# Six weight-half buffers at places of their own modulo 128 bytes, and MLP activations 1024 bytes apart

## The chip, the cores and the metric

The kernel runs on one NeuronCore of a Trainium2 chip. The metric is the device time of one execution in microseconds, as the median of several executions. The profile shown here is one further execution, taken by the hardware profiler.

Names of engines: PE (TensorE: matmuls, and "PEld", its weight loads), DVE (VectorE), ACT (ScalarE), POOL (GpSimd), SP (SyncE, which here only issues DMAs). SBUF is the on-chip memory of 128 partitions; an address below is a byte address within a partition. PSUM holds matmul results.

## The reference

One encoder block over a batch of one, 256 tokens of width 2048. Only the matrix products matter for this change:

```python
mod = jax.nn.silu(c) @ w_ada[l] + b_ada[l]
h = modulate(rms_norm(x, g_norm1[l]), sh1, sc1)
... = jnp.split(h @ w_in[l], IN_SPLITS, axis=-1)      # 2048 -> 7184 columns
...                                                   # mLSTM heads, neighbourhood attention
mixed = jnp.concatenate([h_a, h_b], axis=-1) @ w_out[l]   # 2048 -> 2048
x = x + ga1[:, None, :] * mixed
h = modulate(rms_norm(x, g_norm2[l]), sh2, sc2)
u, g = jnp.split(h @ w_up, 2, axis=-1)                # 2048 -> 2 x 5632
g = ...                                               # depthwise conv of width 3
x = x + ga2 * ((gelu(g) * u) @ w_down)                # 5632 -> 2048
```

Everything is float32 and the result must have float32 accuracy.

## The kernel before

**Split products.** A float32 product is computed from two halves of each operand. `wh` is the weight rounded to the PE's fp32r type, `wl = w - wh` is the rest; an activation is split the same way into `hh` and `hl` (in the down-projection: `aTh` and `aTl`). Each tile product is three one-pass matmuls: high weight by high activation, high weight by low activation, low weight by high activation (L394, L395, L396 in `mm_w`). In `mm_w` the weight slice of 128x128 is the operand that is loaded into the array (PEld) and the activation, 128x256, is the moving operand that streams through it. In `mm_x` (L401 to L403, used only for the two value projections) it is the other way round: the activation is loaded and a row of the weight half, 128x512, streams.

**The weight stream.** All of `w_in`, `w_out`, `w_up` and `w_down` pass once through SBUF, in 391 pieces of up to 128x1024 floats. The class `Stream` does for each piece: SP issues the DMA into a raw buffer `wr` (L349), ACT makes `wh` by a rounding copy (L359), DVE makes `wl` by a subtraction (L367), PE runs the piece's matmuls (24 for most), and then the pair of halves is free again. There are three `wh` and three `wl` buffers (`WH_BUFS = 3`): ACT may be at most three pieces ahead of PE. In this version each trio is a ring of three buffers of 4096 bytes.

**The stages in order.** First `w_in` (until about 388 us of the profile), with the mLSTM and attention work beside it; then `w_out` (to about 487 us); then the up-projection (`second_half`, 4224 matmuls of form L394 to L396 with 256 columns); then the down-projection (`rows` with `down_steps`), from 972 us to 1220 us, and a short tail. In the down-projection 44 activation tiles of 128x256 meet four groups of output columns. The first 40 of them (`n_own`) lie in two large tiles, `aTh` and `aTl`, in which a row is `S + STEP = 260` floats, that is 1040 bytes from one activation to the next. The last four lie in the rings `hh` and `hl`, 1024 bytes apart, as all activations of the earlier stages do. Beside the weight stream runs the modulation matrix `w_ada`, streamed on POOL's queue and reduced on DVE, until about 720 us.

**What sets the order.** A planner (`Sched`) decides at build time in which order each engine's instructions stand. It uses durations and due times, and no addresses.

**Places.** A pool lays its tiles out one after the other, in the order in which they are first asked for. `shift`, a tile of 64 bytes at the start of `wpool`, moves all that follows by 64 bytes. The lines that the change touches:

```python
SHIFT = 16
STEP = 4
wh = self.view(wpool.tile([P, PIECE], F32R, name="wh", tag="wh", bufs=WH_BUFS), nk)
wl = self.view(wpool.tile([P, PIECE], F32R, name="wl", tag="wl", bufs=WH_BUFS), nk)
aTh = upool.tile([P, n_own, S + STEP], F32R, name="aTh")
```

Of the kernel before, what the change touches and what calls it, by code (L numbers as in the profile page):

```python
# [8 lines left out]
F32R = mybir.dt.float32r  # L9
# [5 lines left out]
P = 128  # L15
D = 2048
KT = D // P
S = 256
# [8 lines left out]
FT = FF // P  # L27
# [14 lines left out]
WH_BUFS = 3  # L42
# [26 lines left out]
SEEDS = (0, 1, 1, 1, 1)  # L69
CH = 512  # L70
SHIFT = 16
STEP = 4
PIECE = 1024

CHUNK_COLS = {}
# [69 lines left out]
def block_kernel(ctx, tc, xT_d, cols_d, bg_d, rpb_d, ada_d, win_d, wg_d, wout_d, wup_d, wdown_d, const_d, out_d):  # L145
# [6 lines left out]
    wpool = ctx.enter_context(tc.tile_pool(name="wpool", bufs=1))  # L152
# [22 lines left out]
    class Sched:  # L175
        LAT = {"PE": 0.2, "DVE": 0.14, "ACT": 0.14, "SP": 0.0, "POOL": 0.0}

        def __init__(self):
            self.clock = {"PE": 0.0, "DVE": 0.0, "ACT": 0.0, "SP": 0.0, "POOL": 0.0}
            self.dma_free = 0.0  # L180
            self.chains = []
            self.now = 0.0
            self.slack = 0
# [63 lines left out]
    def held(what):  # L247
        return any(a in flags and b not in flags and what in c for a, b, c in HOLDS)
# [4 lines left out]
    def dve(n, *conds):  # L253
        return "DVE", 0.07 + n / 960, conds

    def act(n, *conds):
        return "ACT", 0.1 + n / 1210, conds
# [65 lines left out]


    class Stream:
        def __init__(self):
            self.todo, self.raw, self.cut, self.half = [], {}, {}, {}
            self.at = {}
            self.pos = 0
            self.wr, self.wh = Ring("wr", WR_BUFS, WR_EARLY), Slots(WH_BUFS)  # L330
# [21 lines left out]
        def cutting(self):  # L352
            for i, (_, _, nk) in enumerate(self.todo):
                n = nk * CH
                t = yield act(n, lambda: self.raw[i][1] if i in self.raw else None, self.wh.has())
                self.wh.take()
                raw = self.view(self.raw[i][0], nk)
                wh = self.view(wpool.tile([P, PIECE], F32R, name="wh", tag="wh", bufs=WH_BUFS), nk)
                A.copy(wh, raw)  # L359
                self.half[i] = (raw, wh, t)  # L360

        def rest(self):
            for i, (_, _, nk) in enumerate(self.todo):
                t = yield dve(nk * CH, lambda: self.half[i][2] if i in self.half and not held("r") else None)
                raw, wh, _ = self.half.pop(i)
                wl = self.view(wpool.tile([P, PIECE], F32R, name="wl", tag="wl", bufs=WH_BUFS), nk)
                V.tensor_sub(wl, raw, wh.bitcast(F32))  # L367
                self.raw.pop(i)[2].give(t)
                self.cut[i] = (wh, wl, t)
# [825 lines left out]
    upool = ctx.enter_context(tc.tile_pool(name="upool", bufs=1))  # L1195
# [1 line left out]
    aslots, gslots = Slots(3), Slots(GC_BUFS)  # L1197
    h2 = [None] * KT
    n_own = FT - CH // P
    aTh = upool.tile([P, n_own, S + STEP], F32R, name="aTh")  # L1200
    aTl = upool.tile([P, n_own, S + STEP], F32R, name="aTl")
    aT = [(aTh[:, j, :S], aTl[:, j, :S]) for j in range(n_own)] + [None] * (FT - n_own)
    cw0, cb0 = NCOL["cw"][0], NCOL["cb"][0]
    gated = {}

# [225 lines left out]
```

## Time and profile before

| what | value |
|---|---|
| median of 3 executions | 1239.87 us |
| lowest, highest | 1239.19, 1254.86 us |
| the profiled execution, its own time | 1237.55 us |
| its span, first to last instruction | 1235.8 us |
| mean granted TensorE clock in it | 0.992 |
| instructions | 24381 |
| weights and other data read from HBM | 318.85 MB |

The page of the profile gives the busy time of each engine, the same in 40 slices of the span, the DMA queues, the chain of work that ended last, and the costliest groups of instructions. A group's line reads: line of the kernel, engine, operation, output and inputs, shapes, count, then the busy time in us and the mean duration of one in ns, and behind the bar the idle time of the engine just before these instructions and what ended it. Matmuls overlap: one of 256 columns is listed with some 277 ns, yet the next one starts after 113 ns or so. What PE costs is therefore read from the distance of the starts, or from the number of matmuls in a stretch of time (a stretch counts the two that reach into it from before as well). The modelled end of a matmul moves with the start of the next, so the listed duration still shows where the distance grows.

### The profile page before, as it was taken

The numbers are of one execution on the slowest core, as the hardware profiler recorded it, in microseconds if no ns is written. First come the engines' busy times: TensorE is split into PE (matmuls) and PEld (weight loads), VectorE is DVE, ScalarE is ACT, GpSimd is POOL, SyncE is SP. The second block draws the span as 40 slices with busy tenths as digits, with TensorE's granted clock in tenths as the row PEclk, the third lists the DMA queues.
The fourth block names the chain that finished last, engine by engine and source line by source line (L and its number), as shares of the span: only waits on it lengthen the run. The fifth ranks groups of instructions, "written<-read, shape, count | busy, mean of one in ns | idle before, by whom it ended". The sixth has DMA issues, their size and how long they took to land.

```text
span 1235.8 us, 24381 instructions
## 1 busy us (share of the span) xinstructions
PE 1208.4 (98%) x9822; PEld 1171.7 (95%) x9822; DVE 906.3 (73%) x1382; ACT 682.9 (55%) x1027; POOL 110.5 (9%) x208
## 2 busy tenths in 40 slices
PE   8899999999999998999999999999999999999996
PEld 6789999999989998999999999999999999999995
DVE  5999889889999998997666676766766545454543
ACT  5896667758777444555445454544555434343432
POOL 1111111122112211010000000000000000000000
PEclk9999999999999999999999999999999999999998
DMA  8999989998998997797777777767666655655552
GB/s 311 402 373 356 331 298 379 374 298 264 323 311 272 380 348 283 255 372 242 228 231 240 232 228 231 243 226 225 217 190 192 197 184 188 186 188 186 184 187 85
DMA packets 91313, 322.55 MB, mean 261 GB/s; under 512 B 10560, under 2 KB 11072, under 8 KB 91200
## 3 DMA queue, kind: packets, MB, share of 16 engines
q1 hardware_dynamic: 63360, 220.84, 52.3%
q0 software_dynamic: 27840, 100.15, 24.0%
q8 instruction: 77, 1.26, 0.4%
q14 instruction: 36, 0.29, 0.1%
HBM read 318.85 MB, written 2.10 MB: 260 GB/s over the span
## 4 chain that ended last, share of the span: by engine, by line
PE 93%; DMA 3%; ACT 2%; DVE 1%; SPq 0%; issue 0%; DVEq 0%; ACTq 0%
PE acc_u L395 13%; PE acc_u L396 13%; PE acc_u L394 13%; PE acc_r L395 9%; PE acc_r L394 9%; PE acc_r L396 9%; PE acc L394 5%; PE acc L395 5%; PE acc L396 5%; PE acc L403 2%; PE acc L402 2%; PE acc L401 2%; DMA wre<-in_win 2%; PE bank L893 1%; ACT wh L359 1%; DMA wr<-in_win 1%
## 5 line engine op out<-in xcount | busy, mean ns | idle before, releaser
L367 DVE TENSOR_TENSOR wl<-wr,wh 128x1024 fp32r<-128x1024 f32 (+1 forms) x391 | 466.6, 1194 | 260.0 <-ACT wh L359 259.0
L359 ACT CAST wh<-wr 128x1024 fp32r<-128x1024 f32 (+1 forms) x391 | 402.0, 1028 | 426.4 <-PE acc_u L395 196.5
L394 PE MATMUL acc_u<-hh,wh 128*128 128x256 f32 x1408 | 389.8, 277 | 3.4 <-ACT hh L435 3.4
L395 PE MATMUL acc_u<-hl,wh 128*128 128x256 f32 x1408 | 389.7, 277 | 0.1
L396 PE MATMUL acc_u<-hh,wl 128*128 128x256 f32 x1408 | 389.4, 277 | 0.0
L394 PEld LDWEIGHTS acc_u<-hh,wh 128*128 128x128 f32 x1408 | 265.2, 188 | 3.9 <-ACT hh L435 3.9
L395 PEld LDWEIGHTS acc_u<-hl,wh 128*128 128x128 f32 x1408 | 265.2, 188 | 0.4 <-DVE hl L437 0.4
L396 PEld LDWEIGHTS acc_u<-hh,wl 128*128 128x128 f32 x1408 | 265.2, 188 | 0.0
L394 PE MATMUL acc<-hh,wh 128*128 128x256 f32 x640 | 182.9, 286 | 6.8 <-ACT hh L435 2.3
L394 PE MATMUL acc_r<-aTh,wh 128*128 128x256 f32 x640 | 180.2, 282 | 0.0
L395 PE MATMUL acc_r<-aTl,wh 128*128 128x256 f32 x640 | 179.7, 281 | 0.0
L396 PE MATMUL acc_r<-aTh,wl 128*128 128x256 f32 x640 | 179.4, 280 | 0.0
L395 PE MATMUL acc<-hl,wh 128*128 128x256 f32 x640 | 178.1, 278 | 0.1
L396 PE MATMUL acc<-hh,wl 128*128 128x256 f32 x640 | 178.0, 278 | 0.0
L465 POOL DMA_DIRECT2D ar<-in_ada x173 | 91.7, 530 | 682.4 <-DVE modp L492 334.4
L394 PEld LDWEIGHTS acc<-hh,wh 128*128 128x128 f32 x640 | 121.0, 189 | 12.4 <-ACT acc L263 4.3
L395 PEld LDWEIGHTS acc<-hl,wh 128*128 128x128 f32 x640 | 121.0, 189 | 1.1 <-DVE are L460 0.3
L396 PEld LDWEIGHTS acc<-hh,wl 128*128 128x128 f32 x640 | 121.1, 189 | 0.0
L395 PEld LDWEIGHTS acc_r<-aTl,wh 128*128 128x128 f32 x640 | 120.5, 188 | 0.1
L396 PEld LDWEIGHTS acc_r<-aTh,wl 128*128 128x128 f32 x640 | 120.6, 188 | 0.0
L394 PEld LDWEIGHTS acc_r<-aTh,wh 128*128 128x128 f32 x640 | 120.4, 188 | 0.1
L492 DVE CUSTOM_DVE_ANT_0 ar<-ar,srow,modp 128x1024 f32<-128x1024 f32 x87 | 111.2, 1278 | 1.6 <-DMA ar<-in_ada 1.4
(202 smaller groups left out, 1562.7 us busy)
## 6 DMA issues: line engine op xcount, KB each, us to landing
wr<-in_wup SPq DMA_DIRECT2D x176, 512.0 KB, 3.9
ar<-in_ada POOLq DMA_DIRECT2D x173, 512.0 KB, 6.1
wr<-in_wdown SPq DMA_DIRECT2D x88, 512.0 KB, 3.5
wr<-in_win SPq DMA_DIRECT2D x73, 512.0 KB, 6.3
wr<-in_wout SPq DMA_DIRECT2D x32, 512.0 KB, 6.3
wre<-in_win SPq DMA_DIRECT2D x25, 512.0 KB, 5.7
are<-in_ada POOLq DMA_DIRECT2D x15, 512.0 KB, 6.2
wr<-in_win SPq DMA_DIRECT2D x22, 256.0 KB, 5.4
```

The source lines that it names most:

```text
L359: A.copy(wh, raw)
L367: V.tensor_sub(wl, raw, wh.bitcast(F32))
L394: T.matmul(acc[:, n, :], w_h, h[0], start=st, stop=False, skip_group_check=True)
L395: T.matmul(acc[:, n, :], w_h, h[1], start=False, stop=False, skip_group_check=True)
L396: T.matmul(acc[:, n, :], w_l, h[0], start=False, stop=last, skip_group_check=True)
L401: T.matmul(acc[:, t, :], h_h, wh[:, k, :], start=first, stop=False, skip_group_check=True)
L402: T.matmul(acc[:, t, :], h_h, wl[:, k, :], start=False, stop=False, skip_group_check=True)
L403: T.matmul(acc[:, t, :], h_l, wh[:, k, :], start=False, stop=last, skip_group_check=True)
L465: q.dma_start(raw, ada_d[a : a + P * PIECE].rearrange("(p n) -> p n", p=P))
L492: V.tensor_tensor_reduce(raw, raw, srow[:, h * PIECE : (h + 1) * PIECE], 1.0, modp[:, part, k : k + 1] if h else cols[:, c : c + 1], ALU.m ...
L893: T.matmul(nu[1][:, : DH_A + 1], at[d][:, j, :], va[:, u, h, :], start=n == 0, stop=n == len(blocks) - 1)
```

## The change

The two rings become six tiles with a buffer each, `wh0` to `wh2` and `wl0` to `wl2`, taken in turn by the new method `half_tile`. Each is 16 floats longer than a piece, and the piece starts in it after 0, 8, 12 or 16 floats by the table `OFFS`. `aTh` and `aTl` lose the four spare floats of each row.

```diff
-STEP = 4
+OFFS = {"wh": (0, 8, 8), "wl": (16, 12, 12)}
+PAD = 16
...
     class Stream:
+        def half_tile(self, what):
+            q = self.turn[what]
+            self.turn[what] = (q + 1) % WH_BUFS
+            o = OFFS[what][q]
+            return wpool.tile([P, PIECE + PAD], F32R, name=f"{what}{q}", tag=f"{what}{q}", bufs=1)[:, o : o + PIECE]
+
...
+            self.turn = {"wh": 0, "wl": 0}
...
-                wh = self.view(wpool.tile([P, PIECE], F32R, name="wh", tag="wh", bufs=WH_BUFS), nk)
+                wh = self.view(self.half_tile("wh"), nk)
...
-                wl = self.view(wpool.tile([P, PIECE], F32R, name="wl", tag="wl", bufs=WH_BUFS), nk)
+                wl = self.view(self.half_tile("wl"), nk)
...
-    aTh = upool.tile([P, n_own, S + STEP], F32R, name="aTh")
-    aTl = upool.tile([P, n_own, S + STEP], F32R, name="aTl")
-    aT = [(aTh[:, j, :S], aTl[:, j, :S]) for j in range(n_own)] + [None] * (FT - n_own)
+    aTh = upool.tile([P, n_own, S], F32R, name="aTh")
+    aTl = upool.tile([P, n_own, S], F32R, name="aTl")
+    aT = [(aTh[:, j, :], aTl[:, j, :]) for j in range(n_own)] + [None] * (FT - n_own)
```

The planner sees no difference: both programs have the same instructions in the same order on every engine, with the same shapes and the same waits; the ring of three and the three single buffers are reused in the same turn. What differs is where the operands start. The built programs have these places:

| operand | before: start, byte modulo 128 (256) | after: start, byte modulo 128 (256) |
|---|---|---|
| `wh`, buffers 0, 1, 2 | 64, 64, 64 (64, 64, 64) | 64, 96, 32 (64, 224, 32) |
| `wl`, buffers 0, 1, 2 | 64, 64, 64 (64, 64, 64) | 64, 48, 112 (192, 176, 240) |
| `hh`, `hl`, all 32 | 0 (0) | 0 (0), untouched |
| `aTh`, first activation, and step | 0 (128), step 1040 | 0 (0), step 1024 |
| `aTl`, first activation, and step | 0 (0), step 1040 | 0 (0), step 1024 |

A weight slice within a half starts a multiple of 512 bytes behind the half's start, so it has the half's place. `aTl` lies 41600 bytes behind `aTh` before (162 times 256, and 128) and 40960 bytes after (160 times 256); `hl` lies 16384 bytes behind `hh` in both. The buffers `wr` and `h_t` stay where they were; `ar` moves by 384 bytes, the tiles of the first stages by 384.

## Prediction

> **What bounds the kernel.** I read the page first: busy shares, the 40 slices, the chain that ended last.
>
> ```profile
> span 1235.8 us, 24381 instructions
> PE 1208.4 (98%) x9822; PEld 1171.7 (95%) x9822; DVE 906.3 (73%) x1382; ACT 682.9 (55%) x1027; POOL 110.5 (9%) x208
> ...
> PE 93%; DMA 3%; ACT 2%; DVE 1%; SPq 0%; issue 0%; DVEq 0%; ACTq 0%
> PE acc_u L395 13%; PE acc_u L396 13%; PE acc_u L394 13%; PE acc_r L395 9%; PE acc_r L394 9%; PE acc_r L396 9%; PE acc L394 5%; PE acc L395 5%; PE acc L396 5%; PE acc L403 2%; PE acc L402 2%; PE acc L401 2%; DMA wre<-in_win 2%; PE bank L893 1%; ACT wh L359 1%; DMA wr<-in_win 1%
> ```
>
> PE is busy for 98% of the span and makes 93% of the chain, nearly all of it the matmuls of L394 to L396. A PE that never waits can only gain by a smaller distance between its matmuls. So the next view is the busy time by stage: length of the stretch, then busy us and count for PE, PEld, DVE, ACT and POOL, granted clock, DMA share, GB/s.
>
> ```profile
> 20.00:250.00 230.00, 224.25 (x1643) 207.99 (x1644) 206.12 (x299) 172.86 (x269) 39.68 (x75) 0.99 0.96 355
> 390.00:480.00 90.00, 90.00 (x766) 89.11 (x765) 86.77 (x144) 45.14 (x69) 17.22 (x32) 1.00 0.96 351
> 500.00:960.00 460.00, 460.00 (x4062) 460.00 (x4061) 328.56 (x444) 230.68 (x308) 19.54 (x37) 1.00 0.72 237
> 972.40:1028.80 56.40, 56.40 (x481) 56.40 (x481) 27.18 (x28) 22.21 (x24) 0.00 (x0) 1.00 0.58 187
> 1029.00:1034.30 5.30, 5.30 (x49) 5.30 (x48) 2.45 (x2) 2.08 (x2) 0.00 (x0) 1.00 0.63 199
> 1034.50:1090.80 56.30, 56.30 (x481) 56.30 (x480) 27.26 (x27) 23.75 (x28) 0.00 (x0) 1.00 0.61 188
> ```
>
> The up-projection (500 to 960) runs 4060 matmuls in 460 us, 113.3 ns apart (two of the count reach in from before). The down-projection on `aTh` and `aTl` (972.4 to 1028.8) runs 479 in 56.4 us, 117.7 ns apart, at the same granted clock of 1.00 and with no idle time. In between, from 1029.0 to 1034.3, the last four activations stream from the rings `hh` and `hl`: 47 in 5.3 us, 113 ns, with the same weights, engines and DMA around them. The groups by form say the same in the listed durations (the two of `acc_r<-hh` x56 are those of the down stage alone):
>
> ```profile
> L394 PE MATMUL acc_r<-aTh,wh 128*128 128x256 f32 x640 | 180.2, 282 | 0.0
> L395 PE MATMUL acc_r<-aTl,wh 128*128 128x256 f32 x640 | 179.7, 281 | 0.0
> L394 PE MATMUL acc_u<-hh,wh 128*128 128x256 f32 x1408 | 389.8, 277 | 3.4 <-ACT hh L435 3.4
> L394 PE MATMUL acc<-hh,wh 128*128 128x256 f32 x640 | 182.9, 286 | 6.8 <-ACT hh L435 2.3 <-ACT acc L263 2.1 <-ACT r_va L263 1.2
> L394 PE MATMUL acc_r<-hh,wh 128*128 128x256 f32 x320 | 90.1, 282 | 0.0
> ...
> L394 PE MATMUL acc_r<-hh,wh 128*128 128x256 f32 x56 | 15.5, 277 | 0.0
> L395 PE MATMUL acc_r<-hl,wh 128*128 128x256 f32 x56 | 15.5, 276 | 0.0
> ```
>
> So 1920 matmuls (three lines of 640) pay 4.4 ns each for the activation's place alone, 8.4 us together. The other 256-column matmuls of the three lines, 3 x (1408 + 640 + 320) = 7104, are at 113.3 ns in steady flow; waits and restarts lift the means of the first stages (286, 282).
>
> **The slow beat without any change of place.** The timeline of PE in the first stage shows that 117.7 ns is a second rhythm that the same operands can fall into:
>
> ```profile
> 87.22 0.28 PE L395 MATMUL acc<-hl,wh 128*128 128x256 f32 x1
> ...
> 88.28 0.28 PE L395 MATMUL acc<-hl,wh 128*128 128x256 f32 x1
> ...
> 88.64 0.39 PE L394 MATMUL acc<-hh,wh 128*128 128x256 f32 x1
> ...
> 89.34 0.28 PE L396 MATMUL acc<-hh,wl 128*128 128x256 f32 x1
> ...
> 90.02 0.28 PE L396 MATMUL acc<-hh,wl 128*128 128x256 f32 x1
> ```
>
> From 87.22 to 88.28 nine distances make 1.06 us, 117.8 ns; after a pause that ends at 88.64, from 89.34 to 90.02, six make 0.68 us, 113.3 ns. Halves and activations lie at the same places modulo 512 in both. A stream thus keeps the beat that it entered with until it is broken. This is the main unknown of the forecast.
>
> **The change, part by part.** No instruction is added, removed or moved, no DMA grows, no wait is new, so nothing is queued behind anything new on SP, POOL or elsewhere. Four things get another place.
>
> *Activations, 1024 bytes apart.* `aTh` and `aTl` then start at 0 modulo 256 throughout, as `hh` and `hl` do. Nearest row: 1029 to 1034, the rings at 113 ns. Ends: 0 (the place isn't the cause) and 1920 x 4.4 = -8.4 us. I take -8.4, because the row of the rings differs from its neighbours in little but the place.
>
> *Weight halves as the loaded operand (L394 to L396).* Six places instead of one. For the lower end: could 113.3 ns itself be the price of the weight load meeting the moving stream, so that another place makes it less? The gate projection answers, since its loads have 16 columns instead of 128:
>
> ```profile
> L1026 PEld LDWEIGHTS bank<-hh,wgh x16: 94/94/94, 28.0 to 248.4; 128*16 128x16 f32 x16
> ...
> 95.57 0.28 PE L1026 MATMUL bank<-hh,wgh 128*16 128x256 f32 x1
> ...
> 96.14 0.28 PE L1028 MATMUL bank<-hl,wgh 128*16 128x256 f32 x1
> ```
>
> Five distances in 0.57 us: 114 ns by the rounded starts, although the load takes 94 ns where the full one takes 188. So 113.3 isn't made by the load, and I see no gain to be had; lower end 0. Upper end: all 7104 in the slow beat, 7104 x 4.4 = +31.3 us. I take 0: the gate weights lie 64 bytes apart, at two places modulo 128 in turn, and the fast beat lasts through them.
>
> *Weight halves as the moving operand (L401 to L403, 3 x 128 matmuls of 512 columns).*
>
> ```profile
> L401 PE MATMUL acc<-wh,hh 128*128 128x512 f32 x128 | 50.7, 396 | 1.1 <-ACT r_qb L263 0.6 <-ACT acc L263 0.4
> ...
> 128.32 0.39 PE L401 MATMUL acc<-wh,hh 128*128 128x512 f32 x1
> ...
> 129.46 0.39 PE L403 MATMUL acc<-wh,hl 128*128 128x512 f32 x1
> ```
>
> Five distances in 1.14 us are 228 ns, against 2 x 113.3 = 226.6. Ends: -0.5 us if all fall to 226.6, and +3.4 us if they take the slow beat (384 x 226.6 x 4.4 / 113.3). I take 0, nearer to the first.
>
> *ACT and DVE at odd places.* The copies into `wh` and the subtractions now write and read at 32, 48, 96 or 112 modulo 128. The nearest rows are the splits into `aTh` and `aTl`, which before go to eight different places modulo 128, 16 bytes apart (min/median/max in ns):
>
> ```profile
> L1240 DVE TENSOR_TENSOR aTl<-g_c,aTh x40: 417/421/426, 554.2 to 933.9; 128x256 fp32r<-128x256 f32 x40
> L1238 ACT CAST aTh<-g_c x40: 394/402/408, 551.8 to 932.6; 128x256 fp32r<-128x256 f32 x40
> ```
>
> 1% of spread over all places: cost 0. Cover: ACT idles before its `wh` copies for PE to free a half,
>
> ```profile
> L359 ACT CAST wh<-wr 128x1024 fp32r<-128x1024 f32 x369 | 388.3, 1053 | 418.8 <-PE acc_u L395 196.5 <-PE acc_r L395 176.8 <-issue 15.0
> L367 DVE TENSOR_TENSOR wl<-wr,wh 128x1024 fp32r<-128x1024 f32 x369 | 451.7, 1224 | 259.6 <-ACT wh L359 258.7
> ```
>
> and only DVE in the output projection (86.77 of 90 us busy, above) has little slack: 1% there is 0.9 us, its bound.
>
> *What is late next.* With the down stage at 113.3, DMA must bring its pieces 4% faster, 0.58 to 0.60 of its time; ACT's waits for PE shrink and stay waits. Nothing takes the place of what is removed, so the gain should reach the end.
>
> Sum against the profiled execution: 1237.55 - 8.4 = 1229.2 us. That execution lies 2.3 us under the median of the three (1239.87) and 1.6 under the lowest; the same sum from the median is 1231.5. I predict 1230.
>
> **Rivals.**
>
> *The halves' places break the fast beat (slower).* The load alternates `wh`, `wh`, `wl`. Before, the three are at one place; after, they differ by 128 modulo 256 in buffer pair 0 and by 80 modulo 128 in pairs 1 and 2, and the slow activations show what such a step may do, since `aTl` stands 128 modulo 256 from `aTh`. In their stage the loads also stretch (187/188/193 ns), as if load and stream met:
>
> ```profile
> L394 PEld LDWEIGHTS acc_r<-aTh,wh x640: 187/188/193, 972.2 to 1218.7; 128*128 128x128 f32 x160
> ```
>
> Two pairs of three in the slow beat: 7104 x 2/3 x 4.4 = +20.8, and the activations keep a third of their gain, -2.8: 1255.6 us. All three: 1268.9. It decides from 8.4 us / 7104 = 1.2 ns per matmul. Against it stand the gates' weights, but those loads are short.
>
> *Nothing changes.* If the spacing isn't what slows `aTh` and `aTl`, the time stays at 1237 to 1240. For this speaks activation number 8, whose two halves start at 0 modulo 128 even before, like the rings, and which is slow all the same:
>
> ```profile
> 983.64 0.28 PE L394 MATMUL acc_r<-aTh,wh 128*128 128x256 f32 x1
> ...
> 985.06 0.28 PE L394 MATMUL acc_r<-aTh,wh 128*128 128x256 f32 x1
> ```
>
> Its twelve matmuls take 1.42 us, 118 ns each. So the place modulo 128 can't be the whole cause; that high and low half stand 128 apart modulo 256 may be, and this the change removes. The Trainium skill (SBUF — State Buffer, Who interferes with whom) says that "PE and ACT never wait on anyone" and gives matmul stream and weight load a read port each; by that rule no place could matter and the sum would be 1237.55. The trace disagrees at least in part: 117.7 against 113 ns side by side in one stage.
>
> *The new places make the distance shorter than 113.3.* One more step of the size seen, 4.4 ns, on the 3 x 1408 + 3 x 704 = 6336 matmuls of the two MLP stages would take 27.9 us more, to 1201; the first 480 us can't follow, with DMA at 0.96. Against it: the gates, and that no stretch of the trace runs below 113. The Trainium skill (TensorE: Matmul & The Clock Gate, Back-to-back issue gap) has N / 2.4 + 2.5 ns, 109 ns for 256 columns; this trace shows it nowhere for these matmuls, and by it the 7104 and the 1920 would save some 46 us together, an estimate from that page.
>
> **Chances.** The forecast (only the activations gain) 0.45; halves break the beat 0.28; nothing changes 0.17; shorter than 113.3 0.10. The likeliest case by itself: 1225 to 1236. The range for 8 in 10 runs from 1219, which leaves most of the last rival out, to 1259, which takes in two slow pairs of three but not all. 2% of the median, about what a measurement of this kernel can tell from no change, is 24.8 us: under 1215.1 only part of the last rival falls (0.06), over 1264.7 only the first rival with nearly all matmuls slow (0.07), and 0.87 lies between.
>
> **What would show it.** In the profile after: the down stage should count some 499 matmuls in 56.4 us instead of 481, and the groups on `aTh`, `aTl` should list 277 ns; the up stage should stay at 4062 in 460 us. If the up stage counts fewer, the halves' places cost; if it counts more, 113.3 was no floor; if the down stage keeps 481, the spacing was not the cause. The L359 and L367 groups should keep 1053 and 1224 ns. I would be wrong above all if the beat that a stage enters is a matter of its first microsecond: then the up-projection could run slow from end to end, +18.6 us.

## The result, and the profile after

The changed kernel is slower: 1254.31 us median of 18 executions (1252.17 to 1256.11) against 1239.05 of 18 of the kernel before (1236.40 to 1256.36). The ratio is 1.0129, with a 95% interval of 1.0122 to 1.0136. The ratios here leave out executions that lie over 1.5% above the fastest of their kernel; of the kernel before these were 18 of 65 over all comparisons, at 1254.9 to 1258.4 us, and the experiments below show what they are. The profiled execution of the changed kernel took 1253.53 us.

The page of the changed kernel: span, busy time, and the chain that ended last. The three matmul lines are now L402 to L404, the copy into `wh` is L367, the subtraction L375.

```profile
span 1251.8 us, 24381 instructions
...
PE 1225.4 (98%) x9822; PEld 1187.6 (95%) x9822; DVE 907.8 (73%) x1382; ACT 681.4 (54%) x1027; POOL 110.6 (9%) x208
...
PE 94%; ACT 2%; DMA 1%; DVE 1%; issue 0%; DVEq 0%; SPq 0%; ACTq 0%
```

The same instructions, PE still busy for 98% and still nearly the whole chain, and no other engine busier by more than 2 us: PE alone needs 17 us more. The busy time by stage shows where (columns as in the prediction: stretch, length, busy us and count of PE, PEld, DVE, ACT and POOL, granted clock, DMA share, GB/s). The down-projection's first column group now stands at 991 to 1052, its own 40 activations up to 1046.7 and the four from the rings after that.

```profile
390.00:480.00 90.00, 90.00 (x742) 88.75 (x741) 85.43 (x147) 46.16 (x74) 17.28 (x32) 1.00 0.94 338
500.00:960.00 460.00, 460.00 (x3951) 460.00 (x3951) 323.73 (x438) 222.31 (x297) 20.06 (x38) 1.00 0.70 233
991.00:1046.60 55.60, 55.60 (x481) 55.60 (x480) 27.18 (x28) 22.21 (x24) 0.00 (x0) 1.00 0.59 190
1047.00:1052.20 5.20, 5.20 (x47) 5.20 (x47) 2.45 (x2) 1.99 (x2) 0.00 (x0) 1.00 0.65 202
```

The up-projection runs 3949 matmuls in 460 us, 116.5 ns apart, where it ran 4060 at 113.3. The down-projection's own activations run 479 in 55.6 us, 116.1 ns, a little better than the 117.7 of before; the activations from the rings, 113 ns before, stand at 116 too (45 in 5.2 us). In the mean these stages have come to one distance. The granted clock is 1.00 in all four rows, and in the last three PE has no idle time.

The listed durations say the same by group (busy us, mean ns), and that the copies and subtractions did not change:

```profile
L402 PE MATMUL acc_u<-hh,wh 128*128 128x256 f32 x1408 | 394.4, 280 | 3.5 <-ACT hh L443 3.5
L404 PE MATMUL acc_u<-hh,wl 128*128 128x256 f32 x1408 | 392.4, 279 | 0.0
...
L402 PE MATMUL acc_r<-aTh,wh 128*128 128x256 f32 x640 | 179.4, 280 | 0.0
...
L403 PE MATMUL acc_r<-aTl,wh 128*128 128x256 f32 x640 | 177.9, 278 | 0.0
...
L409 PE MATMUL acc<-wh,hh 128*128 128x512 f32 x128 | 51.2, 400 | 1.5 <-ACT r_qb L264 0.8 <-ACT acc L264 0.5 <-ACT r_qa L264 0.2
...
L375 DVE TENSOR_TENSOR wl<-wr,wh 128x1024 fp32r<-128x1024 f32 x369 | 451.6, 1224 | 269.8 <-ACT wh L367 268.0
L367 ACT CAST wh<-wr 128x1024 fp32r<-128x1024 f32 x369 | 387.2, 1050 | 433.8 <-PE acc_u L403 208.3 <-PE acc_r L403 176.9 <-issue 17.2
```

The two timelines show in which stages the 16.0 us between the two profiled executions arise. Below are the first matmul of `w_out`, of the up-projection and of the down-projection, and the last matmul of the down-projection, in the kernel before and then in the changed one (start, listed duration):

```profile
387.21 0.28 PE L394 MATMUL acc_r<-hh,wh 128*128 128x256 f32 x1
491.04 0.58 PE L394 MATMUL acc_u<-hh,wh 128*128 128x256 f32 x1 [3.45 <-ACT hh L435]
972.33 0.28 PE L394 MATMUL acc_r<-aTh,wh 128*128 128x256 f32 x1
1221.83 0.28 PE L396 MATMUL acc_r<-hh,wl 128*128 128x256 f32 x1
```

```profile
391.79 0.28 PE L402 MATMUL acc_r<-hh,wh 128*128 128x256 f32 x1
497.60 0.58 PE L402 MATMUL acc_u<-hh,wh 128*128 128x256 f32 x1 [3.46 <-ACT hh L443]
990.96 0.28 PE L402 MATMUL acc_r<-aTh,wh 128*128 128x256 f32 x1
1237.82 0.28 PE L404 MATMUL acc_r<-hh,wl 128*128 128x256 f32 x1
```

They stand 4.6, 6.6, 18.6 and 16.0 us later. So the input projection costs 4.6, `w_out` 2.0, the up-projection 12.1 more, and the down-projection gives 2.6 back. These are single executions: in the profiles below of the kernels whose high halves stand 64 bytes from `hh` as before, `w_out` begins between 386.3 and 388.9 us, so the 4.6 is known to a microsecond or two only.

The timeline of PE shows how 116.5 is made. Rows: start, listed duration, engine, line, operation. Of three pieces in turn, on the buffers `wh2`, `wh0` and `wh1`, the first row of each and a few between are shown:

```profile
700.69 0.28 PE L402 MATMUL acc_u<-hh,wh 128*128 128x256 f32 x1
...
703.50 0.29 PE L402 MATMUL acc_u<-hh,wh 128*128 128x256 f32 x1
...
704.22 0.28 PE L402 MATMUL acc_u<-hh,wh 128*128 128x256 f32 x1
...
704.56 0.28 PE L402 MATMUL acc_u<-hh,wh 128*128 128x256 f32 x1
...
706.26 0.28 PE L402 MATMUL acc_u<-hh,wh 128*128 128x256 f32 x1
...
709.07 0.28 PE L402 MATMUL acc_u<-hh,wh 128*128 128x256 f32 x1
```

Each piece has 24 matmuls. On `wh2` (700.69 to 703.50) they take 2.81 us, 117.1 ns each, and on `wh1` (706.26 to 709.07) the same. On `wh0` (703.50 to 706.26) the first six take 0.72 us, 120 ns each, but from 704.56 on fifteen take 1.70 us, 113.3 ns: within the piece PE finds back to the fast beat, without a pause, and loses it again with the next buffer. The whole up-projection does so in a turn of three pieces: mean distances by buffer pair are 115.0 (pair 0), 116.8 (pair 1) and 117.1 ns (pair 2).

### The profile page after: what moved, and what is told of

Same layout as the page of the kernel before. It is cut to its first block, busy times and chain, and to the rows that moved or that the text cites. A ratio compares the mean times of both kernels' runs of the same rounds, so it can differ in the third digit from the quotient of the medians.

```text
span 1251.8 us, 24381 instructions
## 1 busy us (share of the span) xinstructions
PE 1225.4 (98%) x9822; PEld 1187.6 (95%) x9822; DVE 907.8 (73%) x1382; ACT 681.4 (54%) x1027; POOL 110.6 (9%) x208
## 4 chain that ended last, share of the span: by engine, by line
PE 94%; ACT 2%; DMA 1%; DVE 1%; issue 0%; DVEq 0%; SPq 0%; ACTq 0%
PE acc_u L402 13%; PE acc_u L404 13%; PE acc_u L403 13%; PE acc_r L402 9%; PE acc_r L404 9%; PE acc_r L403 9%; PE acc L402 6%; PE acc L404 5%; PE acc L403 5%; PE acc L409 2%; PE acc L411 2%; PE acc L410 2%; PE bank L901 1%; ACT wh L367 1%; DMA wr<-in_win 1%; PE bank L861 1%
## 5 line engine op out<-in xcount | busy, mean ns | idle before, releaser
L375 DVE TENSOR_TENSOR wl<-wr,wh 128x1024 fp32r<-128x1024 f32 (+1 forms) x391 | 466.5, 1194 | 270.5 <-ACT wh L367 268.7
L367 ACT CAST wh<-wr 128x1024 fp32r<-128x1024 f32 (+1 forms) x391 | 401.0, 1026 | 441.2 <-PE acc_u L403 208.3
L402 PE MATMUL acc_u<-hh,wh 128*128 128x256 f32 x1408 | 394.4, 280 | 3.5 <-ACT hh L443 3.5
L404 PE MATMUL acc_u<-hh,wl 128*128 128x256 f32 x1408 | 392.4, 279 | 0.0
L402 PEld LDWEIGHTS acc_u<-hh,wh 128*128 128x128 f32 x1408 | 264.9, 188 | 3.9 <-ACT hh L443 3.9
L404 PEld LDWEIGHTS acc_u<-hh,wl 128*128 128x128 f32 x1408 | 265.2, 188 | 0.0
L402 PE MATMUL acc<-hh,wh 128*128 128x256 f32 x640 | 184.4, 288 | 5.9 <-ACT hh L443 2.3
L402 PE MATMUL acc_r<-aTh,wh 128*128 128x256 f32 x640 | 179.4, 280 | 0.0
L404 PE MATMUL acc<-hh,wl 128*128 128x256 f32 x640 | 178.7, 279 | 0.0
L404 PE MATMUL acc_r<-aTh,wl 128*128 128x256 f32 x640 | 178.1, 278 | 0.0
L402 PEld LDWEIGHTS acc<-hh,wh 128*128 128x128 f32 x640 | 120.8, 189 | 11.6 <-ACT acc L264 4.0
L403 PEld LDWEIGHTS acc<-hl,wh 128*128 128x128 f32 x640 | 120.9, 189 | 1.0 <-DVE are L468 0.2
L404 PEld LDWEIGHTS acc<-hh,wl 128*128 128x128 f32 x640 | 120.8, 189 | 0.0
L404 PEld LDWEIGHTS acc_r<-aTh,wl 128*128 128x128 f32 x640 | 120.2, 188 | 0.0
L402 PEld LDWEIGHTS acc_r<-aTh,wh 128*128 128x128 f32 x640 | 120.1, 188 | 0.1
```

The costliest lines, as they stand in the source:

```text
L402: T.matmul(acc[:, n, :], w_h, h[0], start=st, stop=False, skip_group_check=True)
L403: T.matmul(acc[:, n, :], w_h, h[1], start=False, stop=False, skip_group_check=True)
L404: T.matmul(acc[:, n, :], w_l, h[0], start=False, stop=last, skip_group_check=True)
```

## The experiments

Places are start bytes modulo 256. "Distance" between a half and an activation means the half's place minus the activation's, modulo 256; the kernel before has 64 for all halves against `hh` and `hl`. In none of the kernels does an instruction, its order or a wait differ; only places do. A "beat" is a distance between starts that stays from matmul to matmul; a "pause" is a longer distance, over 130 ns, that breaks the steady flow.

**The spacing alone.** The kernel before, with the step of 1040 bytes made 1024.

```diff
-STEP = 4
+STEP = 0
```

> The kernel before with STEP = 0, so the activations lie 1024 bytes apart and nothing else is changed (halves in their rings, all at 64 modulo 128). Theory P (the place of the halves is what costs, the spacing of the activations gains): the down stage falls from 117.7 to 113.3 ns per matmul, 1920 x 4.4 = 8.4 us less than the kernel before, about 1230.5 us. Rival S (the spacing gains nothing by itself): 1239 us, down stage at 117.7.

Measured: 1237.58 us against 1238.58, ratio 0.9998 (0.9987 to 1.0009). The spacing alone gains nothing. The windows of its profile, up-projection, own activations of the down-projection, and rings:

```profile
500.00:960.00 460.00, 460.00 (x4061) 460.00 (x4060) 328.80 (x444) 231.25 (x308) 19.54 (x37) 1.00 0.71 237
971.60:1028.00 56.40, 56.40 (x481) 56.40 (x480) 27.17 (x28) 22.16 (x24) 0.00 (x0) 1.00 0.57 187
1028.10:1033.30 5.20, 5.20 (x48) 5.20 (x47) 2.45 (x2) 2.10 (x2) 0.00 (x0) 1.00 0.60 203
```

The activations, now 1024 apart, still run 479 in 56.4 us, 117.7 ns. In this kernel `aTh` and `aTl` both start at 128 modulo 256, while in the changed kernel both start at 0. They stand 1024 apart, and at 0 modulo 128, in both. So if anything of the activations' place matters, it is a place modulo 256. The last row is the first of five stretches on the rings. In three of the five the distance falls to 113 ns within four matmuls of the change from `aTh` to `hh`, without a pause (46 in 5.2 us). In the last two, each behind a pause in this stage, it stays slow; the fourth, from its first matmul to the next one on `aTh`:

```profile
1186.12 0.28 PE L394 MATMUL acc_r<-hh,wh 128*128 128x256 f32 x1
...
1188.95 0.28 PE L394 MATMUL acc_r<-aTh,wh 128*128 128x256 f32 x1
```

Its 24 distances make 2.83 us, 117.9 ns each.

**The parts of the change apart.** First the six single buffers with all halves at 64 modulo 128 and the activations 1024 apart, at 0 modulo 256:

```diff
-OFFS = {"wh": (0, 8, 8), "wl": (16, 12, 12)}
-PAD = 16
+GAPS = {'wlb': 64, 'end': 64}
...
-            o = OFFS[what][q]
-            return wpool.tile([P, PIECE + PAD], F32R, name=f"{what}{q}", tag=f"{what}{q}", bufs=1)[:, o : o + PIECE]
+            n = what + "abc"[q]
+            if GAPS.get(n):
+                wpool.tile([P, GAPS.pop(n) // 4], F32, name="gap_" + n, tag="gap_" + n)
+            half = wpool.tile([P, PIECE], F32R, name=n, tag=n, bufs=1)
...
+            return half
```

> The changed kernel, but its six single buffers all start at 64 modulo 128 (small unused tiles between them set that). Theory P: as e1, about 1230.5 us, all stages at 113.3 ns. Rival B (the buffers cost as such, being six and lying apart, whatever their place modulo 128): 1254 us, as the changed kernel.

Measured: 1228.90 us (1226.87 to 1230.36, 4 executions), ratio 0.9930 (0.9905 to 0.9955). Its windows:

```profile
500.00:960.00 460.00, 460.00 (x4062) 460.00 (x4061) 328.43 (x443) 230.35 (x307) 19.54 (x37) 1.00 0.71 237
972.60:1026.80 54.20, 54.20 (x481) 54.20 (x480) 27.18 (x28) 22.24 (x24) 0.00 (x0) 1.00 0.61 194
```

4060 in 460 us and 479 in 54.2 us: 113.3 and 113.2 ns. This is what the prediction had in mind for the change as made. Second, the changed kernel with the step of 1040 bytes put back:

```diff
+STEP = 4
...
-    aTh = upool.tile([P, n_own, S], F32R, name="aTh")
+    aTh = upool.tile([P, n_own, S + STEP], F32R, name="aTh")
```

> The changed kernel with STEP = 4 back, so only the halves' places are changed. Theory P: the three earlier stages at 116.3 ns as in the changed kernel, the down stage at 117 to 118: 1254.3 + 1920 x 1.4 = about 1257 us. Rival A (it is the activations at 1024 bytes that cost, in all stages by some later effect): near 1239.

Measured: 1256.49 us, ratio 1.0155 (1.0135 to 1.0175), the up-projection at 116.6 ns (3945 in 460 us) and the activations at 118.0 (478 in 56.4):

```profile
500.00:960.00 460.00, 460.00 (x3947) 460.00 (x3946) 322.82 (x437) 222.33 (x297) 20.06 (x38) 1.00 0.70 232
991.10:1047.50 56.40, 56.40 (x480) 56.40 (x480) 27.18 (x28) 22.23 (x24) 0.00 (x0) 1.00 0.56 187
```

So six single buffers cost nothing and the halves' places cost all. Of the activations' new place only some 2 us are left while the halves are spread (1256.49 against 1254.31).

**Is it the step between high and low half?** Three pairs, in each of which the high and the low half stand at the same place modulo 128, but the pairs at different ones; modulo 256 (96, 96), (128, 0) and (160, 32).

```diff
-GAPS = {'wlb': 64, 'end': 64}
+GAPS = {'wha': 32, 'whb': 32, 'whc': 32, 'wlb': 32, 'wlc': 32, 'end': 96}
```

> The changed kernel with the two halves of a piece at one place: pair a both at 96 modulo 128, pair b both at 0, pair c both at 32. If a pair only has to be at one place, whichever (theory U), each pair settles at 113.3 ns within six matmuls of its 24, mean near 114.5, about 1239 us. If it has to be 64 bytes from the activations (theory D), all three pairs run at 116 to 118 ns: 9024 x 3.5 over the best, about 1262 us.

Measured: 1275.68 us in one execution. A row of its `w_out` stage, and the groups of one line on the three high halves:

```profile
420.00:475.00 55.00, 55.00 (x460) 54.89 (x460) 49.72 (x76) 24.50 (x32) 9.31 (x18) 1.00 0.96 351
```

```profile
L406 PE MATMUL acc_u<-hh,whc 128*128 128x256 f32 x472 | 134.0, 284 | 3.5 <-ACT hh L447 3.5
...
L406 PE MATMUL acc_u<-hh,wha 128*128 128x256 f32 x472 | 132.5, 281 | 0.0
...
L406 PE MATMUL acc_u<-hh,whb 128*128 128x256 f32 x464 | 130.4, 281 | 0.0
```

458 matmuls in 55 us, 120.1 ns, and the listed durations of all three are at the slow beat's 281 or above (the fast beat's are 276 to 277). In the up-projection the distances are 118.8, 118.1 and 120.9 ns by pair. No unbroken stretch of twelve or more distances ahead of the up-projection averages under 117 ns. So equal places modulo 128 within a pair do not help. Modulo 256 only the first pair has no step, and it stands in turn with the others; whether the step from `wh` to `wl`, which the first rival took for the danger, is the cause is settled by two kernels below, one with all halves at 192 and one with the low halves at 192. The cost is above what was expected, since the third pair is slower than the slow beat of before. (Here the activations of the down stage start at 128 modulo 256; the argument rests on the stages ahead of it.)

**Both activations at 0 modulo 256, the rings untouched.** A gap of 128 bytes ahead of `aTh` in the kernel of the first experiment.

```diff
-STEP = 4
+STEP = 0
...
+    upool.tile([P, 32], F32, name="gap_a", tag="gap_a")
     aTh = upool.tile([P, n_own, S + STEP], F32R, name="aTh")
```

> The kernel before with STEP = 0 as in e1, and 128 unused bytes ahead of aTh, so that aTh and aTl start at 0 modulo 256 instead of 128; halves in their rings at 64. Theory Q (the place of the streaming activations counts modulo 256, that of the weight halves modulo 128): the down stage at 113.3 ns, about 1229 us as e2. Rival V (it was the spread-out single buffers of e2 that let the down stage run fast): down stage at 117.7, 1237 us as e1.

Measured: four executions at 1229.38 to 1230.90 us and one, the profiled one, at 1256.87; ratio of the four 0.9934 (0.9917 to 0.9952). That is the gain of the activations, and with the first experiment it shows that it hangs on 128 bytes. The one execution is as instructive. Its `w_out` stage and its up-projection:

```profile
420.00:475.00 55.00, 55.00 (x487) 55.00 (x487) 52.88 (x83) 25.51 (x33) 8.71 (x17) 1.00 0.96 356
500.00:960.00 460.00, 460.00 (x3908) 460.00 (x3907) 318.73 (x429) 219.43 (x293) 19.54 (x37) 1.00 0.68 230
```

113.4 ns up to 475 us, and 117.8 (3906 in 460) in the up-projection, at a granted clock of 1.00 and on operands that stand as in the other four. The slow beat begins at 496 us, five us into the stage, where its steady flow begins, and holds for 5844 matmuls without a break. 5844 x 4.4 is 25.7 us, of the 26.9 that this execution has over the others. The kernel before has the same two outcomes: its 18 executions of 65 near 1257 lie some 18.5 us above the others, and 4224 x 4.4 = 18.6 is the up-projection in the slow beat (its down-projection is slow in either case). No profile of such an execution of the kernel before was taken, so for it this is inferred.

**Place or distance, modulo 128 or 256?** Two kernels. Both have the step of 1024 bytes. One moves all halves (and the raw buffers) by 128 bytes, to 192 modulo 256, which leaves the place modulo 128; the activations stand at 0 in all stages. The other leaves the distance at 64 and moves both sides by 64 bytes.

```diff
-STEP = 4
+STEP = 0
...
         def cutting(self):
+            wpool.tile([P, 32], F32, name="gap_w", tag="gap_w")
```

> As e8, but all six halves (and the raw buffers) 128 bytes further, at 192 modulo 256, the activations at 0 modulo 256 in all stages. Theory Q (for the halves only the place modulo 128 counts): all stages at 113.3 ns, about 1229 us. Rival M (what counts is the distance of half and activation modulo 256, which is then what it is in e1's slow down stage): all stages at 117 to 118 ns, 9024 x 4.4 = about 1268 us.

```diff
-STEP = 4
+STEP = 0
...
     wpool = ctx.enter_context(tc.tile_pool(name="wpool", bufs=1))
+    ring.tile([P, 16], F32, name="gap_r", tag="gap_r")
...
+    upool.tile([P, 32], F32, name="gap_a", tag="gap_a")
```

> As e8, with everything from the activation rings on moved by 64 bytes: activations at 64 modulo 256, halves at 128. Distance theory (only the distance between the streaming and the loaded operand counts): all stages at 113.3 ns, about 1229 us. Place theory (the streaming operand must itself start at 0 modulo 256): all stages at 116 to 118 ns, 1255 to 1268 us.

Measured, one execution each: 1267.54 us for the first and 1232.48 for the second. The first's `w_out` stage and up-projection, then the second's up-projection and down-projection:

```profile
420.00:475.00 55.00, 55.00 (x466) 54.89 (x465) 50.41 (x77) 24.68 (x33) 9.50 (x18) 1.00 0.95 355
520.00:960.00 440.00, 440.00 (x3739) 440.00 (x3738) 304.42 (x408) 209.48 (x281) 19.52 (x37) 1.00 0.69 231
```

```profile
500.00:960.00 460.00, 460.00 (x4061) 460.00 (x4060) 328.67 (x444) 230.96 (x308) 20.07 (x38) 1.00 0.70 237
980.00:1010.00 30.00, 30.00 (x267) 30.00 (x266) 13.88 (x13) 11.94 (x13) 0.00 (x0) 1.00 0.57 193
```

With all halves at distance 192 the two windows run at 118.5 and 117.7 ns (464 in 55 with its short pauses, 3737 in 440). With both sides moved, 113.3 (4059 in 460) and 113.2 (265 in 30). What the second kernel has over 1230 is one slow episode of 513 matmuls in `w_out`, from 418 us on, that a pause ended.

One execution each would be little, since a stage can take either beat. But ahead of the up-projection each of these executions has some 35 unbroken stretches of twelve or more distances, and most keep one beat from end to end. Those with a mean under 115.5 ns are 31 of 36 in the kernel before, 34 of 36 in the one with both activations at 0 (the execution at 1256.87 us), 30 of 36 with both sides moved by 64 bytes, and 3 of 35 with all halves at 192. So it is the distance, modulo 256, that counts, and not either place. But at 192 the fast beat is only seldom taken, not impossible. The longest of the three fast stretches, its first and last matmul:

```profile
97.00 0.28 PE L395 MATMUL acc<-hh,wh 128*128 128x256 f32 x1
...
103.69 0.28 PE L397 MATMUL acc<-hh,wl 128*128 128x256 f32 x1
```

Its 59 distances make 6.69 us, 113.4 ns each.

**All high halves at 64 modulo 128, the low ones elsewhere.** Six buffers, modulo 256 (64, 96), (192, 0), (192, 32).

```diff
-GAPS = {'wlb': 64, 'end': 64}
+GAPS = {'wla': 32, 'whb': 96, 'wlc': 32, 'end': 96}
```

> The changed kernel with the three high halves at 64 modulo 128 and the three low halves at 96, 0 and 32; activations at 0 modulo 256. One load in three is then out of place, so by theory Q each piece loses the fast beat once per three matmuls: all three buffers at 115 to 118 ns, 1245 to 1268 us. Rival H (only the high half, loaded for two of three matmuls, has to be in place): 113.3 ns, about 1229 us.

Measured: 1271.87 us in one execution. By pair the distances in the up-projection are 118.6, 117.8 and 118.0 ns: none is fast, and the time lies above both expectations. The other two pairs have the high half at 192, so only the first tests a high half at 64: with a low half at 96, and in turn with these two, it does not find back to the fast beat within its 24 matmuls, unlike pair 0 of the changed kernel.

**High and low half apart: 64 and 192.** Pair 0 of the changed kernel, (64, 192), found back to the fast beat by itself. In the next kernel all pairs stand so, as two rings, activations at 0; then the six buffers were run again (two of their pairs are (64, 192), one is (64, 64)), and last the other way round, high at 192 and low at 64.

```diff
-STEP = 4
+STEP = 0
...
+                if i == 0:
+                    wpool.tile([P, 32], F32, name="gap_l", tag="gap_l")
                 wl = self.view(wpool.tile([P, PIECE], F32R, name="wl", tag="wl", bufs=WH_BUFS), nk)
```

> Rings as in the kernel before, both activations at 0 modulo 256, the loaded high halves at 64 and the loaded low halves at 192 modulo 256 (before: both at 64). Theory W (a matmul whose high half stands 64 bytes from the streaming activation and whose low half stands 192 from it knows only the fast beat, so the slow beat can't keep itself up): every stage at 113.3 ns per 256-column matmul, median near 1229 us, and none of the runs near 1256. Rival (where the low half stands is without effect on which beat is entered): median near 1229 us too, but about a quarter of the runs (10 of 39 of the kernel before) near 1256. Second rival (the low half has to be at 64 too): 1255 to 1268 us in all runs.

> The same kernel as the six single buffers at 64 modulo 128, run again for more runs. Theory W (two of its three pairs have the low half at 192 modulo 256 from the activation, and end a slow beat within some matmuls): no run near 1255, median 1229 us. Rival (its four runs merely missed the slow beat): about a quarter of the runs near 1255.

```diff
-STEP = 4
+STEP = 0
...
+                if i == 0:
+                    wpool.tile([P, 32], F32, name="gap_h", tag="gap_h")
                 wh = self.view(wpool.tile([P, PIECE], F32R, name="wh", tag="wh", bufs=WH_BUFS), nk)
...
+                if i == 0:
+                    wpool.tile([P, 32], F32, name="gap_l", tag="gap_l")
                 wl = self.view(wpool.tile([P, PIECE], F32R, name="wl", tag="wl", bufs=WH_BUFS), nk)
...
+    upool.tile([P, 32], F32, name="gap_a", tag="gap_a")
```

> Rings, activations at 0 modulo 256, the loaded high halves at 192 and the low halves at 64 modulo 256 (the other way round than in the run with the low halves at 192). If the high half's place decides: the slow beat of 117 to 118 ns in all stages, 1255 to 1268 us. If it is enough that either half stands at 64: 113.3 ns and about 1229 us.

Measured: low at 192, 1229.73 us (1227.97 to 1230.98, 5 executions), ratio 0.9934 (0.9920 to 0.9947). The six buffers, 1229.62 (1226.89 to 1231.05, 6 executions), ratio 0.9932 (0.9918 to 0.9946). High at 192, 1268.00 in one execution. Of the 15 executions of the first two kinds none lies near 1256; with 18 in 65, as in the kernel before, that would happen by chance about once in 130 times ((47/65) to the power of 15 is 0.008). Four of the 15 were known before the expectation was written; for the 11 after it the chance is about 1 in 35. The timeline of the kernel with the low halves at 192, where `w_in`'s matmuls begin anew after those of 512 columns, shows why:

```profile
109.75 0.28 PE L396 MATMUL acc<-hh,wh 128*128 128x256 f32 x1
...
110.71 0.28 PE L398 MATMUL acc<-hh,wl 128*128 128x256 f32 x1
110.82 0.28 PE L396 MATMUL acc<-hh,wh 128*128 128x256 f32 x1
...
112.98 0.28 PE L397 MATMUL acc<-hl,wh 128*128 128x256 f32 x1
```

Eight distances in 0.96 us are 120 ns; the next nineteen, 110.82 to 112.98, are 113.7. The stage is entered in the slow beat and leaves it after three turns of the three matmuls, without a pause. In this profile 21 of 28 slow episodes of eight or more distances (counted where the mean of three in turn is over 115.6 ns) end so, none after more than some 13, and a pause cuts the other seven. In the kernel before all nine such episodes ahead of the down-projection lasted until a pause. The up-projection itself is entered in the slow beat in this execution, at the same point as in the execution at 1256.87 us above, and leaves it:

```profile
496.54 0.28 PE L397 MATMUL acc_u<-hl,wh 128*128 128x256 f32 x1
...
497.49 0.28 PE L396 MATMUL acc_u<-hh,wh 128*128 128x256 f32 x1
...
498.51 0.28 PE L396 MATMUL acc_u<-hh,wh 128*128 128x256 f32 x1
```

Eight distances in 0.95 us are 119 ns, the next nine in 1.02 us 113.3, and the stage stays there. With the low halves at 64 the slow beat entered at 496 us had held for 5844 matmuls.

The kernel with the high halves at 192, `w_out` and up-projection:

```profile
420.00:475.00 55.00, 55.00 (x486) 54.95 (x486) 52.80 (x83) 25.41 (x33) 8.98 (x17) 1.00 0.96 356
500.00:960.00 460.00, 460.00 (x3867) 460.00 (x3867) 317.37 (x430) 218.37 (x294) 20.06 (x38) 1.00 0.69 228
```

484 in 55 us are 113.6 ns, 3865 in 460 us are 119.0 (118.9 from 501 us on, where the steady flow begins), at unchanged places. Neither expectation held: the place allows the fast beat, and allows a slow one, of 118.9, that keeps itself up. So the same kernel was run again.

> The kernel of the run with the loaded high halves at 192 modulo 256, five rounds instead of one look. Its one run held 113.3 ns in the first stages and from 420 to 475 us, and the slow beat from 501 us to the end, at unchanged places. Theory B (with these places both beats keep themselves up, and the up-projection's first matmuls pick one): two groups of times, one near 1230 us and one near 1268 us, none between 1240 and 1260. Theory H (the high half's place decides): all runs at 1255 to 1270 us.

Measured in 10 executions: four at 1232.30 to 1235.92 us and six at 1262.81 to 1266.26, none between; the median of all, 1263.29, describes neither group (the four have a ratio of 0.9964, 0.9950 to 0.9979, to the kernel before). The profiled one is of the four; the same two windows:

```profile
420.00:475.00 55.00, 55.00 (x488) 55.00 (x487) 52.79 (x83) 25.03 (x32) 9.54 (x18) 1.00 0.96 357
500.00:960.00 460.00, 460.00 (x4061) 460.00 (x4061) 328.18 (x443) 230.47 (x309) 20.04 (x38) 1.00 0.71 237
```

Here the up-projection runs at 113.3 ns (4059 in 460). One program, one clock, two beats: up to 6336 matmuls (up- and down-projection) x 5.6 ns = 35.5 us are decided when the up-projection begins, and the two groups lie 27 to 34 us apart.

Together, by the distance of high and low half from the streaming activation:

| distance of (high, low) half | where | ns per matmul of 256 columns |
|---|---|---|
| (64, 64) | before, `w_in` to up; both activations at 0; all moved by 64 | 113.3, or 117.8 until a pause |
| (64, 192) | low halves at 192; pair 0 of the changed kernel | 113.3; a slow beat ends by itself |
| (192, 64) | high halves at 192 | 113.3, or 118.9 until a pause |
| (192, 192) | all halves at 192; spacing alone, down stage | 117.8; seldom 113.3 (3 of 35 stretches) |
| (224, 176), (32, 240) | pairs 1 and 2 of the changed kernel | 116.8, 117.1 |
| (96, 96), (128, 0), (160, 32) | three pairs | 118.8, 118.1, 120.9 |
| (64, 96), (192, 0), (192, 32) | high halves at 64 modulo 128 | 118.6, 117.8, 118.0 |

The last three rows are of pairs that stand in turn with one another, so what a pair would do alone is not shown by them. Left open: by what mechanism the chip makes the distance matter; what at the start of a stage picks one of two beats; and why in the spacing-alone kernel the rings, at (64, 64), return to 113 ns straight after slow activations in three stretches and keep the slow beat in the other two. Whether a place modulo 512 or more counts beside that modulo 256 was not tried by itself.

## Why the prediction was wrong, point by point

The prediction said 1230, the run 1254; the likeliest case was wrong, and the outcome of the first rival came true, at nearly its price, though not for its reason.

*The step that failed: the weight halves as the loaded operand.* It was put between 0 and +31.3 us and taken at 0, "the gate weights lie 64 bytes apart, at two places modulo 128 in turn, and the fast beat lasts through them". Measured, it is +4.6 (input projection, with the 0.8 of the moving operand in it), +2.0 (`w_out`) and +12.1 (up-projection), 18.6 us together: the fast beat does not last through halves at these places. The row on the gates was read rightly and was no evidence: those loads take 94 ns of a distance of 113, those of the halves 188, longer than the distance itself. That the length of the load is what makes the gates immune is likely, but no run shows it. The prediction named that very doubt ("but those loads are short") and gave it too little weight. The distance table shows that full loads at two places can even keep the fast beat, (64, 192), but only at the right places.

*The activations.* The term of -8.4 has the right size and was tied to the wrong thing. The spacing alone gains nothing (ratio 0.9998); at 0 modulo 256 beside halves at 64 it gains 0.66% (0.9934), 8.2 us of 1239. In the changed kernel only 2.6 us of it are left, because the halves no longer stand at 64 in two pairs of three. The rival "nothing changes" was right that the place modulo 128 isn't the cause and that one modulo 256 may be. Its own candidate, high and low activation 128 apart, is not the cause by itself: in the spacing-alone kernel both start at 128 modulo 256, and the stage is as slow.

*The first rival.* It gave 1255.6, +20.8 and -2.8. Measured: 1254.3; +18.6 by the starts of the stages up to the down-projection, and -2.6 in it. That the sum comes so near is in part luck: it had two pairs at 117.7 and one at 113.3, and they run at 117.1, 116.8 and 115.0, pair 0 being slow for its first six matmuls of each piece. Its reason, a step between `wh` and `wl`, fell: halves without a step are slow (all at 192) and halves with a step of 128 are fast (low halves at 192).

*The moving operand.* Taken at 0 between -0.5 and +3.4; the listed 396 ns became 400, and by the starts, waits left out, the distance of the 384 matmuls went from 229.0 to 231.1 ns, 0.8 us. Inside its bounds.

*ACT and DVE at odd places.* Right: 1053 and 1050 ns for the copy, 1224 and 1224 for the subtraction. (The row on ACT that it was read from spans 394 to 408 ns, more than the 1% that was read; the copies show no such spread in the mean.)

*What is late next.* Right as far as it could be tested: PE is never idle in the late windows, also not in the six-buffer kernel, with the down stage at 113.2 ns and DMA at 0.61.

*The warning at the end*, that the beat a stage enters may be a matter of its first microsecond and then cost 18.6 us, describes something real: the 117.8 ns of one execution from 496 us on, and the two groups of the kernel with the high halves at 192. But the changed kernel's 18 executions form one group; their loss is not chance, it is the places.

*The two rules.* By the Trainium skill (SBUF — State Buffer, Who interferes with whom), under which weight load and stream have a port each, no place could matter; here places alone move the distance from 113.3 to 120.9 ns. The formula in the Trainium skill (TensorE: Matmul & The Clock Gate, Back-to-back issue gap), which the section gives for an isolated matmul, makes 109 ns of 256 columns; the best steady window of any kernel here is 113.2.

## What to carry to other kernels

Where one-pass fp32r matmuls with full 128x128 loads run back to back, the byte distance modulo 256 between the loaded weight and the streaming activation is a tuning parameter worth 4% of PE time: set every buffer's place on purpose (here the high half 64 past the activation, the low half 64 or better 192 past it), and do not spread them. Only multiples of 32 bytes and a few of 16 were tried here. When a kernel's times fall into two groups, profile one of each: here the same program keeps one of two beats, and with the low halves, all or two of three, moved by 128 bytes none of 15 executions fell into the slow group. A row that acquits a suspect must share the property that makes it suspect; loads of 16 columns say nothing of loads of 128.

The kernels with six buffers at 64 modulo 128, or with rings and the low halves at 192, beat both versions: 1229.6 and 1229.7 us, 0.7% under the kernel before, which was measured beside them, and 2.0% under the changed one, which was not (1229.6 / 1254.31 = 0.980).

## What the runs showed of the hardware that was not expected

- Which distance back-to-back matmuls keep depends on the distance of two SBUF addresses modulo 256, not on either place: at 64, also with both sides moved by 64 bytes, 30 to 34 of 36 stretches run near 113.3 ns; at 192, 32 of 35 run at 117.8.
- PE has two beats for the same operands, 113.3 and 117.8 ns at (64, 64), and 113.3 and 118.9 at (192, 64), at a granted clock of 1.00. The slow one can last 5844 matmuls.
- With (64, 192) the slow beat ends by itself, after at most some 13 matmuls in the kernel that has it throughout; times then have one group (1226.9 to 1231.1 in 15 executions of two kernels).
